# First layer's attention: the context values and probabilities split into high and low parts, and 512 keys in one product

## The chip, the cores and the metric

The kernel runs on one core of a Trainium2 chip. The metric is device microseconds of one execution. TensorE (PE in the profile) multiplies into PSUM, VectorE (DVE) and ScalarE (ACT) read PSUM and SBUF, SyncE's queue (SP) issues the transfers.

## The reference, cut to what matters

Two layers of a block with three token mixers (a gated linear recurrence, an mLSTM, a windowed attention), 512 latent tokens and 256 context tokens, width 2048, all in fp32. Only the attention is touched. It has 8 query heads of 128 channels; four heads share one key and value head (two of these).

```python
# latent tokens: a window of 128 to each side, and all 256 context keys
s_loc = einsum('bnqkgd,bnskd->bnkgqs', qb, kw) * scale      # masked to the window
s_ctx = einsum('bnqkgd,bckd->bnkgqc', qb, k_ctx) * scale
p = softmax(concatenate([s_loc, s_ctx, s_sink], axis=-1))
out = p[..., :span] @ vw + p[..., span:span + n_ctx] @ v_ctx
# context tokens (first layer only): the 256 context keys alone, and the sink
```

The result is `out * silu(cz)`. The context tokens' own attention is wanted in the first layer only, since the second layer is the last.

## The kernel before

**Layout.** Activations stand with channels on the 128 partitions and tokens along the free dimension: 512 latent tokens, two spare columns, 256 context tokens. A chunk is 128 tokens: 0 to 3 are latent, 4 and 5 context. Every projection (class `Proj`, method `mm`, L359) multiplies a 128-column weight tile by 512 and by 258 columns of activations, 16 times (the 16 slices of the width) and three times each: operands are cut into a high part of type fp32r and the rest, and high x high, high x low and low x high are summed. `load_w` (L318 to L322) fetches weights, ScalarE writes the high part, VectorE the low one; there are four buffers of each.

**The attention of one head** (`unit_c`): the query is projected, rotated (`rope`, its scratch tile from a ring of two buffers, tag `e`) and cut into two parts (`halves`, L1031 and L1032); then `attend` is called for three pairs of chunks. In the first layer these are (0, 3), (1, 4) and (2, 5), so there are 24 calls; in the second layer (0, 3), (1), (2). A latent chunk at the edge (0, 3) sees two local blocks of 128 keys, one in the middle (1, 2) three, a context chunk none; each sees the two context blocks, numbered 4 and 5.

**Inside `attend`:**
- the scores (L1051), three products of fp32r parts for each stretch of keys, into one PSUM tile `scps` of 1024 columns, the only buffer of its pool;
- the mask (L1057), row maximum (L1061), exponentials (L1070), their sum and its inverse, and the scaling of the probabilities `pr` (L1077);
- one transposition on TensorE for each chunk and block (L1084), four to a PSUM tile `ptps`, each tile copied to SBUF by ScalarE (L1085, tile `pt`, ring of two buffers, tag `z`);
- the values times the transposed probabilities, in fp32, one product of 128 columns for each chunk and block (L1091), into the PSUM tile `ops`; `ptps` and `ops` rotate through one pool of two buffers;
- the product with the gate on VectorE (L1093).

`values` turns the value head's 768 tokens so that keys stand on the partitions (`to_tokens`: transpositions at L635, ScalarE's copies at L636), into the tile `lvc`.

**Order.** Each engine's order of instructions is fixed when the program is built, by a planner that simulates the engines' times. It puts the attention's small pieces between the products of the projections that follow. Each engine then runs its list in that order and waits on semaphores.

Of the kernel before, what the change touches and what calls it, by code (L numbers as in the profile page):

```python
# [8 lines left out]
F32 = mybir.dt.float32  # L9
F32R = mybir.dt.float32r  # L10
I32 = mybir.dt.int32
AF = mybir.ActivationFunctionType
ALU = mybir.AluOpType
AX = mybir.AxisListType

P = 128
D = 2048
KT = 16
NL = 512
NC = 256  # L20
NT = NL + NC
XW = NL + 2 + NC
CO = NL + 2
# [5 lines left out]
COLP = [0, 128, 256, 384, CO, CO + 128]  # L29
# [26 lines left out]
def emit(tc, I, out, cfg=None, dbg=None):  # L56
# [5 lines left out]
    V, S, G, T = nc.vector, nc.scalar, nc.gpsimd, nc.tensor  # L62
# [8 lines left out]
    def sps(n, name):  # L71
        return psS.tile([P, 512], F32, tag="s", name=name)[:, 0:n]
# [22 lines left out]
    C_ = {}  # L95
# [438 lines left out]
    def run_units(l, last, up, mods):  # L534
# [5 lines left out]
        def U(i, name):  # L540
            return up.tile([P, 776], F32, tag=f"u{i}", name=name)

        def PAIR(i, name):
            return up.tile([P, 2, 776], F32, tag=f"p{i}", name=name)

        def Z(name):
            return up.tile([P, 776], F32, tag="z", name=name, bufs=2)
# [4 lines left out]
        def small(tag, n, bufs=2):  # L552
            return up.tile([P, n], F32, tag=tag, name=tag, bufs=bufs)
# [22 lines left out]
        def evac(nm, p, dst, extra=None, bias=True):  # L576

            with tc.high_priority():
                return evac_(nm, p, dst, extra, bias)
# [32 lines left out]
        def width(nm):  # L612
            return NL if is_lat(nm) else XW
# [10 lines left out]
        def to_tokens(src, dst, chunks, width_=P):  # L624

            two = isinstance(dst, list) and len(dst) == 2
            dst = dst if isinstance(dst, list) else [dst]
            for i, g in enumerate((chunks[0:4], chunks[4:6])):
                if not g:
                    continue  # L630
                t, c0 = (dst[i], g[0]) if two else (dst[0], 0)
                d = t[:, 0:(g[-1] + 1 - c0) * width_].rearrange("p (c w) -> p c w", w=width_)
                ps = sps(len(g) * P, "tps")
                for j, c in enumerate(g):
                    T.transpose(ps[:, j * P:j * P + P], src[:, COLP[c]:COLP[c] + P], C_["ident"])  # L635
                S.copy(out=d[:, g[0] - c0:g[0] - c0 + len(g), 0:P], in_=ps.rearrange("p (c w) -> p c w", w=P))  # L636

        ALLC = [0, 1, 2, 3, 4, 5]
# [396 lines left out]
        def every(t, c0, step, n, w=P):  # L1035

            return bass.AP(tensor=t.tensor, offset=t.offset + c0, ap=[tuple(t.ap[0]), (step, n), (1, w)])

        def attend(h, cs, q, kr, vt, m):


            n_ = len(cs)
            ps = psW.tile([P, 1024], F32, tag="w", name="scps")
            loc = [[b for b in (c - 1, c, c + 1) if 0 <= b < 4] if c < 4 else [] for c in cs]
            ns = [len(x) * P for x in loc]
            c0s = [512 - ns[0] if ns[0] > 256 else 0, 512 + NC if ns[0] > 256 else 512]
            w = [ps[:, c0:c0 + n + NC] for c0, n in zip(c0s, ns)]
            for c, x, lc, n in zip(cs, w, loc, ns):
                for k0, d0, len_ in ([(lc[0] * P, 0, n)] if lc else []) + [(CO, n, NC)]:
                    for i, (a, b) in enumerate(((0, 0), (0, 1), (1, 0))):  # L1050
                        T.matmul(x[:, d0:d0 + len_], q[:, a, COLP[c]:COLP[c] + P], kr[:, b, k0:k0 + len_],  # L1051
                                 start=(i == 0), stop=(i == 2))
            if ns[0] > 256:
                x, mask = every(w[0], 0, 2 * P, 2), C_["cmask"]
            else:
                x, mask = every(ps, P, 512 - P, 2), C_["cmask"][:, ::-1]
            V.tensor_tensor(out=x, in0=x, in1=mask, op=ALU.add)  # L1057
            sm = small("sm", 8, 4)
            mx, bi, su, si = (sm[:, 2 * i:2 * i + n_] for i in range(4))
            if n_ == 2 and ns[0] == ns[1]:  # L1060
                V.tensor_reduce(out=mx, in_=ps.rearrange("p (c k) -> p c k", c=2), axis=AX.X, op=ALU.max)  # L1061
            else:
                for i in range(n_):
                    V.tensor_reduce(out=mx[:, i:i + 1], in_=w[i], axis=AX.X, op=ALU.max)
            V.tensor_scalar(out=bi, in0=mx, scalar1=-SCALE, scalar2=C_["nsink"][:, l, h:h + 1],
                            op0=ALU.mult, op1=ALU.min)
            prs = []
            for i in range(n_):
                pr = U(8 + i, "pr")[:, 0:ns[i] + NC]
                S.activation(out=pr, in_=w[i], func=AF.Exp, scale=SCALE, bias=bi[:, i:i + 1],  # L1070
                             accum_out=su[:, i:i + 1])
                prs.append(pr)
            S.activation(out=si, in_=bi, func=AF.Exp, bias=C_["sink"][:, l, h:h + 1])
            V.tensor_tensor(out=su, in0=su, in1=si, op=ALU.add)
            V.reciprocal(out=su, in_=su)
            for i, pr in enumerate(prs):
                V.tensor_scalar(out=pr, in0=pr, scalar1=su[:, i:i + 1], scalar2=None, op0=ALU.mult)  # L1077
            blocks = [(i, j, kb) for i in range(n_) for j, kb in enumerate(loc[i] + [4, 5])]
            pts = []
            for a in range(0, len(blocks), 4):  # L1080
                g = blocks[a:a + 4]
                tp, pt = sps(len(g) * P, "ptps"), Z("pt")
                for k, (i, j, kb) in enumerate(g):
                    T.transpose(tp[:, k * P:k * P + P], prs[i][:, j * P:j * P + P], C_["ident"])  # L1084
                S.copy(out=pt[:, 0:len(g) * P], in_=tp)  # L1085
                pts += [pt[:, k * P:k * P + P] for k in range(len(g))]
            o = sps(n_ * P, "ops")
            for i in range(n_):
                mine = [(kb, pt) for (i_, _, kb), pt in zip(blocks, pts) if i_ == i]
                for k, (kb, pt) in enumerate(mine):  # L1090
                    T.matmul(o[:, i * P:i * P + P], vt[kb], pt, start=(k == 0), stop=(k == len(mine) - 1))  # L1091
            d = every(m, COLP[cs[0]], COLP[cs[-1]] - COLP[cs[0]] if n_ > 1 else P, n_)
            V.tensor_tensor(out=d, in0=o.rearrange("p (c k) -> p c k", k=P), in1=d, op=ALU.mult)  # L1093

        def unit_c():
            CS = PAIR(1, "cs")
            cosT, sinT = CS[:, 0, 0:NL], CS[:, 1, 0:NL]
            nc.sync.dma_start(cosT, I["cosT"])
            nc.sync.dma_start(sinT, I["sinT"])

            def values(g):
                nm = f"cv{g}"
                z = evac(nm, proj(nm), None if nm in early else U(5, "zcv"))
                if g == 0 or not last:
                    ts = [small("lvc", 1280, 1)[:, 0:NT]]
                else:
                    ts = [wp.tile([P, 512], F32, tag="st", name="cvt", bufs=7)[:, 0:n] for n in (NL, NC)]
                to_tokens(z, ts, ALLC)
                return [t[:, c:c + P] for t in ts for c in range(0, t.shape[1], P)]

            vts = []
            for h in range(8):
                g = h // 4
                if h % 4 == 0:
                    nm = f"ck{g}"
                    z = evac(nm, proj(nm), None if nm in early else U(7, "zck"))
                    rope(z, cosT, sinT)
                    kr = halves(z, 0, "ckr", XW)
                    vt = vts.pop(0) if vts else values(g)
                    if f"cv1" in ready:  # L1120
                        vts.append(values(1))
                nm, zn = f"cq{h}", f"cz{h}"
                q = evac(nm, proj(nm), None if nm in early else U((7, 5)[h % 2], "cq"))
                rope(q, cosT, sinT)
                q = halves(q, 2, "cqr", width(nm))
                m = evac(zn, proj(zn), None if zn in early else U(10 + h % 2, "cz"), bias=False)
                silu_bias(zn, m)
                for cs in ((0, 3), (1,), (2,)) if last else ((0, 3), (1, 4), (2, 5)):
                    attend(h, cs, q, kr, vt, m)
                nc.sync.dma_start(mixd[l][8 + h][:, 0:NL], m[:, 0:NL])  # L1130
                if not last:
                    nc.sync.dma_start(mixd[l][8 + h][:, NL:NT], m[:, CO:XW])
# [257 lines left out]
    for l in range(layers):  # L1390
        last = l == DEPTH - 1
# [131 lines left out]
```

## Time and profile before

| | us |
|---|---|
| time, median of 3 runs | 2804.38 (2802.26 to 2804.62) |
| the profiled execution | 2807.49 |
| its span | 2805.8 |
| TensorE busy | 2765.3 (99%) |
| VectorE busy | 1818.8 (65%) |
| ScalarE busy | 1180.6 (42%) |

The profile is of one execution, 2807.49 us long, some 3 us above the median. Busy times are inside its span. A matmul's row has a duration that reaches past the start of the next one, since matmuls are pipelined; what a matmul costs a full TensorE is the distance from its start to the next start. An fp32 product leaves two matmul records, an fp32r product and a transposition one. PEld is the load of the stationary operand, which runs beside the products.

### The profile page before, as it was taken

To read this page: it belongs to the slowest core of one execution; us is meant where nothing else is said; L and a number is where in the kernel's file an instruction comes from. 1 tells how busy PE (TensorE), PEld (TensorE's weight loads), DVE (VectorE), ACT (ScalarE), POOL (GpSimd) and SP (SyncE) were. 2 spreads that over 40 slices of the span, in tenths; PEclk is the share of its full clock that TensorE was granted. 3 is DMA by queue.
4 is the path that set the end of the run, shared out by engine and by line. 5 is a ranking of instruction groups with operands and counts; after the bars stand their busy time and mean duration, and the time that the engine had idled before them with its cause. 6 is when DMAs were issued, how large, how long until landed. Compare 5 with 4: busy or idle time off the path is not lost.

```text
span 2805.8 us, 53654 instructions
## 1 busy us (share of the span) xinstructions
PE 2765.3 (99%) x20833; PEld 2483.1 (88%) x20833; DVE 1818.8 (65%) x4163; ACT 1180.6 (42%) x2716; POOL 17.6 (1%) x32
## 2 busy tenths in 40 slices
PE   7999999999999999999999999999999999999998
PEld 4679879988888888889999999999899999999886
DVE  3436556764667778788777778566666665645526
ACT  3314324364453433324666644444444443333433
POOL 0000000000000000000000000000000000000000
PEclk8999999999999999999999999999999999999999
DMA  9771553321113144444767756224222222422535
GB/s 344 257 234 54 168 193 92 119 64 59 54 59 123 56 131 130 126 136 125 235 197 204 231 164 212 67 74 136 79 63 69 65 69 91 140 78 81 176 118 158
DMA packets 208144, 366.74 MB, mean 131 GB/s; under 512 B 24561, under 2 KB 42241, under 8 KB 207761
## 3 DMA queue, kind: packets, MB, share of 16 engines
q1 hardware_dynamic: 207888, 363.31, 41.1%
q8 instruction: 163, 2.67, 0.4%
q14 instruction: 93, 0.75, 0.1%
HBM read 344.94 MB, written 18.28 MB: 129 GB/s over the span
## 4 chain that ended last, share of the span: by engine, by line
PE 91%; DVE 2%; ACT 2%; DMA 1%; issue 1%; DVEq 0%; ACTq 0%; SPq 0%
PE pp L359 70%; PE pp L1345 6%; PE ops L1091 3%; PE scps L1051 2%; PE ptps L1084 1%; PE lv L799 1%; PE modps L246 1%; PE aops L885 1%; DMA raw<-in_wout 1%; PE tps L635 1%; PE sps L867 1%; PE nps L978 1%; PE cps L958 1%; PE nps L976 1%; PE ktps L851 0%
## 5 line engine op out<-in xcount | busy, mean ns | idle before, releaser
L359 PE MATMUL pp<-x0h,hi 128*128 128x256 f32 (+2 forms) x3088 | 942.2, 335 | 7.2 <-ACT x0h L410 5.2
L359 PE MATMUL pp<-x0l,hi 128*128 128x256 f32 (+2 forms) x3088 | 934.8, 332 | 0.1
L359 PE MATMUL pp<-x0h,lo 128*128 128x256 f32 (+1 forms) x3056 | 923.0, 332 | 0.7 <-DVE lo L322 0.7
L321 ACT CAST hi<-raw 128x512 fp32r<-128x512 f32 x764 | 473.0, 620 | 1042.8 <-PE pp L359 760.8
L322 DVE TENSOR_TENSOR lo<-raw,hi 128x512 fp32r<-128x512 f32 x764 | 526.6, 691 | 447.2 <-ACT hi L321 431.4
L359 PEld LDWEIGHTS pp<-x0h,hi 128*128 128x128 f32 x3088 | 544.8, 189 | 69.9 <-issue 6.9
L359 PEld LDWEIGHTS pp<-x0l,hi 128*128 128x128 f32 x3088 | 543.8, 189 | 59.2 <-issue 4.4
L359 PEld LDWEIGHTS pp<-x0h,lo 128*128 128x128 f32 x3056 | 537.1, 189 | 55.4 <-issue 2.5
L359 PE MATMUL pp<-x1h,hi 128*128 128x258 f32 (+1 forms) x1632 | 463.2, 284 | 1.4 <-ACT hi L321 1.3
L359 PE MATMUL pp<-x1l,hi 128*128 128x258 f32 (+1 forms) x1632 | 463.4, 284 | 0.1
L359 PE MATMUL pp<-x1h,lo 128*128 128x258 f32 (+1 forms) x1600 | 454.1, 284 | 0.6 <-DVE lo L322 0.4
L359 PEld LDWEIGHTS pp<-x1h,hi 128*128 128x128 f32 x1632 | 311.1, 191 | 7.8 <-issue 4.4
L359 PEld LDWEIGHTS pp<-x1l,hi 128*128 128x128 f32 x1632 | 309.2, 189 | 4.5 <-issue 3.6
L359 PEld LDWEIGHTS pp<-x1h,lo 128*128 128x128 f32 x1600 | 303.2, 190 | 6.5 <-issue 5.2
L270 DVE SCALAR_TENSOR_TENSOR mo<-st,sc,mo 128x512 f32<-128x512 f32 x150 | 112.8, 752 | 0.5
L270 DVE SCALAR_TENSOR_TENSOR scs<-st,sc,scs 128x512 f32<-128x512 f32 x150 | 112.8, 752 | 0.3
L1345 PE MATMUL pp<-lo,x0h 128*128 128x512 f32 x256 | 101.4, 396 | 0.0
L1345 PE MATMUL pp<-hi,x0h 128*128 128x512 f32 x256 | 100.9, 396 | 0.0
L1345 PE MATMUL pp<-hi,x0l 128*128 128x512 f32 x256 | 100.8, 395 | 0.0
L1085 ACT COPY pt<-ptps 128x512 f32<-128x512 f32 x96 | 47.7, 516 | 122.6 <-PE ptps L1084 122.0
L813 ACT COPY lvc<-aqq 128x256 f32<-128x256 f32 x140 | 60.3, 431 | 84.3 <-DVE aqq L822 63.4
L819 DVE TENSOR_TENSOR akk<-akk,aff 128x256 f32<-128x256 f32 x168 | 76.5, 455 | 12.2 <-PE ktps L851 9.4
(381 smaller groups left out, 3006.4 us busy)
## 6 DMA issues: line engine op xcount, KB each, us to landing
raw<-in_win SPq DMA_DIRECT2D x500, 256.0 KB, 2.7
st<-in_wmod SPq DMA_DIRECT2D x288, 256.0 KB, 3.4
raw<-in_wout SPq DMA_DIRECT2D x192, 256.0 KB, 3.3
mw<-in_wmod SPq DMA_DIRECT2D x96, 256.0 KB, 5.2
raw<-in_wlast SPq DMA_DIRECT2D x80, 256.0 KB, 3.1
st<-in_win SPq DMA_DIRECT2D x24, 256.0 KB, 4.5
xr<-in_xin SPq DMA_DIRECT2D x48, 128.0 KB, 3.3
st<-mixd SPq DMA_DIRECT2D x45, 128.0 KB, 2.7
```

The costliest lines, as they stand in the source:

```text
L246: prev = T.matmul(ps[32 * j:32 * j + 32, :], scs[:, 32 * kt:32 * kt + 32], ws[j], start=(i == 0 and (side or g == 0)), stop=(i == 1 and (s ...
L270: V.scalar_tensor_tensor(out=acc, in0=w, scalar=c, in1=acc, op0=ALU.mult, op1=ALU.add)
L321: S.copy(out=hi, in_=raw)
L322: lo_ins[:] = [V.tensor_tensor(out=lo, in0=raw, in1=hi.bitcast(F32), op=ALU.subtract).ins]
L359: T.matmul(dst, self.w[w][:, kt % 4, :], xs[o][kt][j][:, x0:x0 + n], start=(first and i == 0 and (self.outs is None or self.outs[k][1])), ...
L635: T.transpose(ps[:, j * P:j * P + P], src[:, COLP[c]:COLP[c] + P], C_["ident"])
L813: S.copy(out=mixed(qm.unsqueeze(1), 0, 256, b, 0), in_=mixed(Q2, c0, 256, b))
L819: V.tensor_tensor(out=x, in0=x, in1=blocks(F2, c0, b, b, 776, True), op=ALU.mult)
L1051: T.matmul(x[:, d0:d0 + len_], q[:, a, COLP[c]:COLP[c] + P], kr[:, b, k0:k0 + len_], start=(i == 0), stop=(i == 2))
L1085: S.copy(out=pt[:, 0:len(g) * P], in_=tp)
L1091: T.matmul(o[:, i * P:i * P + P], vt[kb], pt, start=(k == 0), stop=(k == len(mine) - 1))
L1345: x = T.matmul(ps[c], xs[0][kt][a][:, c * P:c * P + P], w[b].rearrange("p a b -> p (a b)"), start=(kt == kts[0] and i == 0), stop=(kt == k ...
```

## The change

In the first layer (`not last`), and nowhere else:

- **Scores.** For a chunk with 256 local keys (chunks 0 and 3) the local and the context keys, two stretches of 256 columns, become the moving operand of one product of 512 columns: 6 products in place of 12 in the call (0, 3). The other two calls keep theirs.
- **Context values.** `values` transposes the same six chunks, but the two context blocks get a PSUM tile, a copy into an fp32r high part and a VectorE subtraction for the low part (tile `vc`); the four local blocks go to `lvc` as before.
- **Context probabilities.** The four transpositions of the two context blocks for both chunks of a call go first, into one PSUM tile, block by block with the two chunks side by side. ScalarE copies it into an fp32r high part (tag `z`), VectorE subtracts for the low part (`ptl`, tag `e`, the ring that `rope` and the gates' scratch use too). The local blocks are transposed and copied after it as before.
- **Values times probabilities.** For each context block three fp32r products of 256 columns (both chunks at once) take the place of two fp32 products of 128 columns. They come first into `ops`; the local blocks' fp32 products add to them.

```diff
-                for k0, d0, len_ in ([(lc[0] * P, 0, n)] if lc else []) + [(CO, n, NC)]:
+                for k0, d0, len_ in [(lc[0] * P, 0, 2 * NC)] if n == NC else ([(lc[0] * P, 0, n)] if lc else []) + [(CO, n, NC)]:
                     for i, (a, b) in enumerate(((0, 0), (0, 1), (1, 0))):
-                        T.matmul(x[:, d0:d0 + len_], q[:, a, COLP[c]:COLP[c] + P], kr[:, b, k0:k0 + len_],
+                        keys = every(kr[:, b], k0, CO - k0, 2, NC) if n == NC else kr[:, b, k0:k0 + len_]
+                        T.matmul(x[:, d0:d0 + len_], q[:, a, COLP[c]:COLP[c] + P], keys,
                                  start=(i == 0), stop=(i == 2))
...
-            blocks = [(i, j, kb) for i in range(n_) for j, kb in enumerate(loc[i] + [4, 5])]
+            blocks = [(i, j, kb) for i in range(n_) for j, kb in enumerate(loc[i] + ([4, 5] if last else []))]
             pts = []
+            if not last:
+                tp = sps(4 * P, "ptps")
+                for k in range(2):
+                    for i in range(2):
+                        j = len(loc[i]) + k
+                        T.transpose(tp[:, (2 * k + i) * P:(2 * k + i) * P + P], prs[i][:, j * P:j * P + P], C_["ident"])
+                both = up.tile([P, 776], F32R, tag="z", name="pt", bufs=2), up.tile([P, 776], F32R, tag="e", name="ptl", bufs=2)
+                S.copy(out=both[0][:, 0:4 * P], in_=tp)
+                V.tensor_tensor(out=both[1][:, 0:4 * P], in0=tp, in1=both[0][:, 0:4 * P].bitcast(F32), op=ALU.subtract)
...
             o = sps(n_ * P, "ops")
+            if not last:
+                for k in range(2):
+                    for j, (a, b) in enumerate(((0, 0), (0, 1), (1, 0))):
+                        T.matmul(o, vt[4 + k][a], both[b][:, 2 * k * P:2 * k * P + 2 * P], start=(k + j == 0),
+                                 stop=(k + j == 3 and not blocks))
...
+                if not last:
+                    t = small("lvc", 1280, 1)
+                    to_tokens(z, t, ALLC[0:4])
+                    ps = sps(NC, "tps")
+                    for j in range(2):
+                        T.transpose(ps[:, j * P:j * P + P], z[:, CO + j * P:CO + j * P + P], C_["ident"])
+                    vc = up.tile([P, 2, NC], F32R, tag="vc", name="vc")
+                    hi, lo = vc[:, 0], vc[:, 1]
+                    S.copy(out=hi, in_=ps)
+                    V.tensor_tensor(out=lo, in0=ps, in1=hi.bitcast(F32), op=ALU.subtract)
```

## Rows read from the trace of the kernel before

**Rows 1.** The page: busy time of each engine, share of the span, instructions.

```profile
PE 2765.3 (99%) x20833; PEld 2483.1 (88%) x20833; DVE 1818.8 (65%) x4163; ACT 1180.6 (42%) x2716; POOL 17.6 (1%) x32
```

**Rows 2.** The chain that ended last, by engine, whole span; then 205 to 570 us.

```profile
PE 91%; DVE 2%; ACT 2%; DMA 1%; issue 1%; DVEq 0%; ACTq 0%; SPq 0%
...
by line: PE pp L359 68.9%; PE ops L1091 10.8%; PE scps L1051 8.7%; PE ptps L1084 5.4%; PE modps L246 4.4%; PE modp L194 0.4%; PE pp L375 0.4%; DVE zg L595 0.3%; PE tps L635 0.3%; ACT Lg L679 0.2%; PE shps L523 0.2%; DVE zg L600 0.1%; issue 
```

**Rows 3.** Busy times by stretch: from:to, length, PE, PEld, DVE, ACT, POOL, clock, DMA.

```profile
210.00:570.00 360.00, 360.00 (x2328) 311.85 (x2329) 220.73 (x455) 131.29 (x268) 1.50 (x2) 1.00 0.39 125
570.00:1340.00 770.00, 766.94 (x5979) 678.75 (x5978) 567.38 (x1325) 321.81 (x859) 9.30 (x16) 1.00 0.31 97
1340.00:1600.00 260.00, 256.00 (x2135) 253.71 (x2135) 198.99 (x475) 167.71 (x361) 0.00 (x0) 1.00 0.72 220
```

**Rows 4.** L1091 and L1051 in 210 to 570 us: records, duration ns min/median/max, forms.

```profile
L1091 PE MATMUL ops<-pt,lvc x352: 269/275/276, 230.3 to 566.1; 128*128 128x128 f32 x176
...
L1051 PE MATMUL scps<-ckr,cqr x240: 275/285/442, 213.8 to 549.7; 128*128 128x256 f32 x96, 128*128 128x384 f32 x24
```

**Rows 5.** Timeline of PE: start, length, engine, line, operation. Twelve scores, then projections.

```profile
213.79 1.60 PE L1051 MATMUL scps<-ckr,cqr 128*128 128x256 f32 x12
...
215.23 0.28 PE L359 MATMUL pp<-x1l,hi 128*128 128x258 f32 x1
```

**Rows 6.** Timeline of PE: the value products of a call, projections around them.

```profile
227.19 0.28 PE L359 MATMUL pp<-x1h,lo 128*128 128x258 f32 x1
227.31 0.39 PE L359 MATMUL pp<-x0h,hi 128*128 128x512 f32 x1
...
230.35 1.95 PE L1091 MATMUL ops<-pt,lvc 128*128 128x128 f32 x16
232.05 0.36 PE L359 MATMUL pp<-x1h,lo 128*128 128x258 f32 x1
232.25 0.40 PE L359 MATMUL pp<-x0h,hi 128*128 128x512 f32 x1
```

**Rows 7.** Timeline of PE, last projection: 512-column fp32r products, first and last of 14.

```profile
2649.77 0.39 PE L1345 MATMUL pp<-hi,x0h 128*128 128x512 f32 x1
...
2652.78 0.39 PE L1345 MATMUL pp<-lo,x0h 128*128 128x512 f32 x1
```

**Rows 8.** DVE by line and shape: count, busy us, mean ns, idle before and releaser.

```profile
L648 DVE TENSOR_TENSOR mix<-mixps,ag 128x512 f32<-128x512 f32 x8 | 5.5, 688 | 14.6 <-PE mixps L646 14.6
L650 DVE TENSOR_TENSOR mix<-mixps,ag 128x256 f32<-128x256 f32 x4 | 1.7, 414 | 0.0
```

**Rows 9.** Timeline, second call of head 0: transpositions, copies, value products.

```profile
235.48 0.93 PE L1084 MATMUL ptps<-c_ident,pr 128*128 128x128 f32 x7
...
240.13 1.72 PE L1091 MATMUL ops<-pt,lvc 128*128 128x128 f32 x14
241.60 1.56 PE L1051 MATMUL scps<-ckr,cqr 128*128 128x256 f32 x11
```

**Rows 10.** Timeline of PE, ACT and DVE, third call: the same, close together.

```profile
243.01 0.60 PE L1084 MATMUL ptps<-c_ident,pr 128*128 128x128 f32 x4
...
243.70 0.59 ACT L1085 COPY pt<-ptps 128x512 f32<-128x512 f32 x1 [4.37 <-PE ptps L1084]
...
244.23 1.23 DVE L1061 TENSOR_REDUCE sm<-scps 128x2 f32<-128x1024 f32 x1
245.62 0.96 DVE L595 TENSOR_TENSOR cq<-pp,rb 128x770 f32<-128x770 f32 x1 [0.17 <-PE pp L359]
...
245.42 1.73 PE L1091 MATMUL ops<-pt,lvc 128*128 128x128 f32 x14
```

**Rows 11.** Waits of PE from 570 to 2800 us: total us, times, longest.

```profile
PE pp L359 <- ACT hi L321: 2.6, 4, 1.1
PE gtps L734 <- ACT PF L724: 2.4, 2, 1.9
PE gtps L734 <- DVE gT L735: 2.3, 2, 1.2
PE pp L359 <- DVE lo L322: 1.1, 3, 0.7
```

**Rows 12.** VectorE's low parts of weights: by shape, and two that follow each other.

```profile
L322 DVE TENSOR_TENSOR lo<-raw,hi 128x512 fp32r<-128x512 f32 x764 | 526.6, 691 | 447.2 <-ACT hi L321 431.4 <-ACT pt L1085 5.9 <-DMA st<-x1d 3.0
...
215.70 0.69 DVE L322 TENSOR_TENSOR lo<-raw,hi 128x512 fp32r<-128x512 f32 x1
...
219.71 0.69 DVE L322 TENSOR_TENSOR lo<-raw,hi 128x512 fp32r<-128x512 f32 x1
```

## What was predicted before the change was run

> **What bounds the kernel now.** I read the engines' busy times first: TensorE is busy for 99% of the span, VectorE for 65%, ScalarE for 42% [rows 1]. The chain that ended last says the same from the other side: 91% of it is TensorE's own work [rows 2]. An average hides stages, so the next view is the stretch in which the first layer's attention runs, 210 to 570 us, by the first and last value product and score [rows 4]: there TensorE is busy for 360.00 of 360.00 us at the full granted clock (1.00, which is 2.4 GHz), while VectorE works 220.73 us and ScalarE 131.29 us and the transfers take 0.39 of the DMA engines [rows 3]. The chain through this stretch is TensorE's lines one after another: the projections' products 68.9%, value products 10.8%, scores 8.7%, transpositions 5.4% [rows 2]. The reader is to see that TensorE never waits here, because the planner has put the attention between projections that are ready anyway. So a microsecond of product time taken out of this stretch is a microsecond off the end, and latency inside the attention costs nothing as long as TensorE has other products in its list. What counts is therefore the price of a product on a full TensorE, which is the distance between starts, not the duration in its row.
>
> **Prices.** Twelve scores of 256 columns take from 213.79 to 215.23 us [rows 5]: 1.44/12 = 0.120 us each. Fourteen starts of 512-column fp32r products lie between 2649.77 and 2652.78 us [rows 7]: 3.01/13 = 0.2315 us each. For the fp32 value product: from the start of the first of 16 records to the second projection product behind them, 230.35 to 232.25 us, there are 1.90 us, and one of the products in between is a 258-column one, which costs 0.12 us (227.19 to 227.31) [rows 6]. So 8 value products cost 1.78 us, 0.2225 us each. I take the distance across the following product because the start of the one behind a group of fp32 records is shifted.
>
> **The change part by part.** *Context values times probabilities:* each of the 24 calls loses four fp32 products, 4 x 0.2225 = 0.890 us, and gets six fp32r products of 256 columns, 6 x 0.120 = 0.720 us. That the row has 352 records, two for each of 8 x (8 + 7 + 7) = 176 products, confirms the count [rows 4]. Gain: 24 x 0.170 = 4.1 us. No row shows an fp32r product with these operands; the nearest are the 256-column scores at 0.120 and the 258-column projections at 0.12, and the best the columns allow is half of the 512-column price, 0.116. With 0.116 the gain is 24 x 0.194 = 4.7 us, with 0.1225 (0.0025 above the scores) it is 24 x 0.155 = 3.7 us. I take 0.120, since the new products also come in a row with one stationary load each, as the scores do.
>
> *Scores of the call (0, 3):* 8 calls lose twelve products of 256 columns, 1.44 us, and get six of 512, 6 x 0.2315 = 1.389 us. Gain: 8 x 0.051 = 0.4 us. The moving operand is now two runs of 256 columns with a gap; no row shows such a product. If each costs what two of 256 do, the gain is 0; if the gap costs as much again as the whole joint saves (0.0085 us a product), it is a loss of 0.4 us. I take the contiguous price: it is the only row of that width.
>
> Here a rule speaks about the size. The Trainium skill, "TensorE: Matmul & The Clock Gate", section "Back-to-back issue gap", gives a gap of N/2.4 + 2.5 ns at full clock, 109.2 ns at 256 columns and 215.8 ns at 512. By that rule an estimate of this edit's gain is 8 x (12 x 0.1092 - 6 x 0.2158) = 0.1 us in place of 0.4. The rows here are dearer (0.120 and 0.2315), and they decide.
>
> *Transpositions:* 8, 7 and 7 before and after; only their order changes. Cost 0.
>
> *ScalarE:* the copies out of `ptps` keep their number (two a call) and their sizes. Cost 0.
>
> *VectorE:* one subtraction of 512 columns out of PSUM more in each call, at the 0.688 us of the nearest form with a PSUM operand, and two of 256 columns at 0.414 us for the values [rows 8]: 24 x 0.688 + 2 x 0.414 = 17.3 us. VectorE is idle for 360.00 - 220.73 = 139 us of the stretch [rows 3], so this I cost at nothing; the work that hides it is the projections' products on TensorE. If that cover were gone it would cost up to 0.688 us in each call (below).
>
> *Waits that are added:* the second of the six products needs the low part, and `ops` needs the buffer that the subtraction is the last to read. On TensorE everything behind that product waits, the next projection's products too. The low parts also take turns in the ring of two that `rope` and the gate's scratch use, so the rotation of the next head's query can start only when the second call's value products are done. That puts some 4 us of rotation and splitting behind them, which TensorE covers with projections that are already in its list. No transfer is added or moved.
>
> **The sum.** 4.1 + 0.4 = 4.5 us, all on TensorE's path. Against the profiled execution: 2807.49 - 4.5 = 2803.0. That execution is 3.1 us above the median of the runs, so in the metric: 2804.38 - 4.5 = 2799.9 us. The bounds of the unknown prices give a gain of 3.7 - 0.4 = 3.3 to 4.7 + 0.4 = 5.1 us, 2799.3 to 2801.1 us. A planner that is given other instructions also orders others differently; I allow 2 us for that to each side: 2797.3 to 2803.0.
>
> **The rivals.**
> *TensorE waits for the low part (slower).* The place is the second context product of each call. In the third call the four transpositions started at 243.01, the copy ended at 243.70 + 0.59 = 244.29, and the first value product started at 245.42 [rows 10]; but VectorE was in a reduction from 244.23 to 245.46. A subtraction behind it would end at about 246.2, so the product, left in its place, would wait some 0.8 us. VectorE's next row starts only at 245.62, behind the reduction [rows 10]. The Trainium skill, "PSUM — Partial Sum Buffer", section "Engine vs sequencer instructions", calls VectorE's queue strict FIFO; by that rule the wait could not be dodged, and the rows agree. At the full price, 0.8 us in all 24 calls, this costs 19 us: 2804.4 - 4.5 + 19 = 2819 us. It makes the kernel slower (by over 5.6 us) from an average wait of (4.5 + 5.6)/24 = 0.42 us a call. Against it: in the second call the transpositions began at 235.48 and the value products only at 240.13 [rows 9], room for the subtraction; and the planner counts the subtraction when it places the products. No value product waits for its copies today.
>
> *The gain is eaten in part.* The same wait in every third call, 8 x 0.6 = 5 us, or a weight's low part late behind VectorE's new work: about 2804.4 us, no change. Against the second: a weight's low part is cast about every 4 us (215.70, 219.71) with 0.691 us of work [rows 12] and four buffers, so VectorE may fall back by some 12 us before TensorE runs out.
>
> *The new order also removes waits elsewhere.* Behind the attention TensorE still waits for parts of weights and for the gates, 2.6 + 2.4 + 2.3 + 1.1 = 8.4 us in all [rows 11]. They depend on how the lists interleave. If half of them go, the time is 2799.9 - 4.2 = 2795.7 us. Against it: nothing in the change aims at them, and new ones are as likely.
>
> *The 512-key product is not one product for the engine.* Then only the 0.4 us is lost: 2800.3 us, inside the forecast's bounds.
>
> **How the numbers follow.** About 0.2%, 5.6 us, is what a measurement of this kernel can tell from no change; faster means below 2798.8 us, slower above 2810.0 us. The forecast (2797.3 to 2803.0) has 0.62, and of that some 0.16 lies below 2798.8. The removed waits (below 2797.3) have 0.16, the eaten gain (2803 to 2810) 0.14, the wait for the low part (above 2810) 0.08. So faster 0.16 + 0.16 = 0.32, same 0.46 + 0.14 = 0.60, slower 0.08. The likeliest is the forecast, 2799.9 us, which lies within 0.2%. The range reaches to half of the removed waits and to the first 2 us of the eaten gain: 2795.7 to 2805.0.
>
> **What would show it right or wrong.** Right: in the first layer's stretch the value products' records fall from 352 to 160, with 144 fp32r ones beside them at 0.120 us from start to start; 48 score records fewer; TensorE still without idle time, and the stretch shorter by 4 to 5 us. Wrong: idle time of TensorE ahead of the context products with the subtraction as releaser; a distance of more than 0.24 us between 512-key scores; or a change of TensorE's waits behind 570 us as large as the gain itself.

## The result, and the profile after

The change made the kernel slower: 2825.83 us (2825.52 to 2827.74) against 2804.38 us, a ratio of 1.0077 with a 95% interval of 1.0067 to 1.0088. That is 21.5 us more where 4.5 us less was forecast.

One statement made ahead of the prediction was wrong: the score edit is not tied to the first layer. It holds wherever a chunk has 256 local keys, so in the second layer's calls (0, 3) too: 16 calls, not 8.

The page of the kernel after, its busy times (as rows 1):

```profile
PE 2772.4 (98%) x20689; PEld 2481.0 (88%) x20689; DVE 1834.3 (65%) x4189; ACT 1180.5 (42%) x2717; POOL 17.6 (1%) x32
```

TensorE has 144 records fewer, as the change says, and yet it is busy for 7 us more. The stretches show where. Busy times of the kernel after, with columns as in rows 3, up to 545 us, through the place of the loss, and behind it:

```profile
210.00:545.00 335.00, 329.58 (x2038) 280.16 (x2037) 193.59 (x390) 117.24 (x238) 0.74 (x1) 0.99 0.36 115
545.00:582.00 37.00, 23.22 (x113) 20.20 (x112) 34.80 (x72) 11.13 (x22) 0.74 (x1) 0.72 0.41 117
582.00:640.00 58.00, 56.74 (x443) 49.01 (x441) 38.99 (x93) 34.79 (x63) 0.00 (x0) 1.00 0.24 74
```

From 545 to 582 us TensorE is busy for 23.22 of 37 us, with a granted clock of 0.72, while VectorE is full (34.80). Most of the loss shows here: counted by the projections' products (L359), the kernel after is 1.7 us ahead of the one before at the 2050th (544.1 against 545.8 us), 22.8 us behind at the 2100th (583.4 against 560.6), and 19 us behind at the end. (The profiled execution of the kernel before was itself 3 us longer than its median.) What TensorE waits for in this stretch (total us, times, longest):

```profile
PE scps L1053 <- ACT pr L1072: 8.8, 1, 8.8
PE ptps L1088 <- DVE pr L1079: 2.3, 2, 1.7
PE ops L1103 <- ACT pt L1097: 1.9, 2, 1.1
PE ops L1103 <- DVE ptl L1091: 0.8, 1, 0.8
```

These are the steps of the last head's calls, one after another: scores wait for exponentials, transpositions for probabilities, value products for copies. The timeline of TensorE there, cut:

```profile
552.55 0.60 PE L194 MATMUL modp<-c_ident,scs 128*128 128x128 f32 x4
561.98 2.61 PE L1053 MATMUL scps<-ckr,cqr 128*128 128x384 f32 x9 [8.82 <-ACT pr L1072]
566.25 0.45 PE L1088 MATMUL ptps<-c_ident,pr 128*128 128x128 f32 x1 [1.67 <-DVE pr L1079]
...
568.98 0.58 PE L1103 MATMUL ops<-pt,vc 128*128 128x256 f32 x1 [0.79 <-ACT pt L1097]
570.34 0.58 PE L1103 MATMUL ops<-ptl,vc 128*128 128x256 f32 x1 [0.77 <-DVE ptl L1091]
...
573.13 2.15 PE L1053 MATMUL scps<-ckr,cqr 128*128 128x384 f32 x9
...
578.41 0.80 PE L359 MATMUL pp<-x0h,hi 128*128 128x512 f32 x1
```

Between 552.55 and 578.41 us there is no projection product at all. In the kernel before the attention's pieces lay between projections [rows 6]; here none is left to run. The reason stands on VectorE's timeline. The last head's query leaves PSUM at 491.32 us, and its rotation starts at 543.23, right behind the third call's subtraction of the head before:

```profile
491.32 0.96 DVE L595 TENSOR_TENSOR cq<-pp,rb 128x770 f32<-128x770 f32 x1
...
539.98 0.42 DVE L1110 TENSOR_TENSOR cz<-ops,cz 128x256 f32<-128x256 f32 x1 [1.74 <-PE ops L1108]
540.39 0.69 DVE L322 TENSOR_TENSOR lo<-raw,hi 128x512 fp32r<-128x512 f32 x1
542.51 0.69 DVE L1091 TENSOR_TENSOR ptl<-ptps,pt 128x512 fp32r<-128x512 f32 x1 [1.43 <-ACT pt L1090]
543.23 0.69 DVE L1023 TENSOR_TENSOR rope<-cq,cs 64x512 f32<-64x512 f32 x1
```

The same query in the kernel before (timeline of VectorE):

```profile
499.72 0.95 DVE L595 TENSOR_TENSOR cq<-pp,rb 128x770 f32<-128x770 f32 x1
...
501.95 0.69 DVE L1023 TENSOR_TENSOR rope<-cq,cs 64x512 f32<-64x512 f32 x1
```

Before, 2.2 us lie between the two; after, 51.9 us. That is not itself the price, since the head before has its own first scores only at 511.15 us. The price stands between two heads: from the third scores of the first head to the first scores of the second there were 8.0 us before (233.64 to 241.60 [rows 9]), and there are 18.1 us after (230.59 to 248.64).

```profile
242.90 0.69 DVE L1091 TENSOR_TENSOR ptl<-ptps,pt 128x512 fp32r<-128x512 f32 x1
243.62 0.69 DVE L1023 TENSOR_TENSOR rope<-cq,cs 64x512 f32<-64x512 f32 x1
248.64 1.22 PE L1053 MATMUL scps<-ckr,cqr 128*128 128x512 f32 x2 [3.48 <-ACT cqr L1031]
```

So the rotation stands behind the third call's subtraction at the first change of head too, and TensorE runs out of work there as well: the projections have no product between 241.58 and 249.66 us. Up to 545 us TensorE is idle for 5.42 us (335.00 less 329.58), 3.48 us of it here; the kernel before had no idle time there [rows 3]. The count of projection products hides this loss, because the attention is later at that count than it was before.

Back to the last head. The next mixer's first query projection is written over the keys' tile (both are the pair with number 0), so it stays in its PSUM buffer until the last scores are done: it leaves at 577.40 us, behind the scores of 573.13.

```profile
577.40 0.95 DVE L595 TENSOR_TENSOR aqq<-pp,rb 128x770 f32<-128x770 f32 x1
```

The gates' projection holds the other buffer of that pool. It leaves by a copy into a tile (`zg`) of the ring in which the turned probabilities stand (tag `z`), and the copy waits for a call's value products:

```profile
594.60 0.80 ACT L372 COPY zg<-pp 128x770 f32<-128x770 f32 x1 [3.50 <-PE ops L1103]
```

So TensorE has no place for a third projection. This is theory R: the ring that the low parts share with the rotation makes the heads follow one another where they used to overlap, the attention falls behind the projections, and the lateness is paid where TensorE's list runs out, above all beside the last head.

### The profile page after: what moved, and what is told of

Read it like the earlier page. It is cut to its first block, busy times and chain, and to the rows that moved or that the text cites. A ratio compares the mean times of both kernels' runs of the same rounds, so it can differ in the third digit from the quotient of the medians.

```text
span 2824.8 us, 53370 instructions
## 1 busy us (share of the span) xinstructions
PE 2772.4 (98%) x20689; PEld 2481.0 (88%) x20689; DVE 1834.3 (65%) x4189; ACT 1180.5 (42%) x2717; POOL 17.6 (1%) x32
## 4 chain that ended last, share of the span: by engine, by line
PE 90%; DVE 3%; ACT 2%; DMA 1%; issue 0%; SPq 0%; DVEq 0%; ACTq 0%
PE pp L359 70%; PE pp L1374 6%; PE scps L1053 2%; PE ops L1108 2%; PE lv L799 1%; PE modps L246 1%; PE aops L885 1%; PE ptps L1096 1%; PE tps L635 1%; PE sps L867 1%; PE nps L978 1%; PE cps L958 1%; PE nps L976 1%; PE ops L1103 1%; PE ktps L851 0%
## 5 line engine op out<-in xcount | busy, mean ns | idle before, releaser
L359 PE MATMUL pp<-x0h,hi 128*128 128x256 f32 (+2 forms) x3088 | 942.2, 335 | 7.1 <-ACT x0h L410 5.1
L359 PE MATMUL pp<-x0l,hi 128*128 128x256 f32 (+2 forms) x3088 | 935.3, 333 | 0.1
L359 PE MATMUL pp<-x0h,lo 128*128 128x256 f32 (+1 forms) x3056 | 922.0, 332 | 0.3 <-DVE lo L322 0.3
L359 PEld LDWEIGHTS pp<-x0h,hi 128*128 128x128 f32 x3088 | 545.6, 189 | 70.7 <-ACT x0h L410 6.8
L359 PEld LDWEIGHTS pp<-x0l,hi 128*128 128x128 f32 x3088 | 544.2, 189 | 60.1 <-issue 5.2
L359 PEld LDWEIGHTS pp<-x0h,lo 128*128 128x128 f32 x3056 | 537.1, 189 | 54.6 <-issue 1.7
L359 PE MATMUL pp<-x1h,hi 128*128 128x258 f32 (+1 forms) x1632 | 463.7, 285 | 0.2 <-ACT hi L321 0.2
L359 PE MATMUL pp<-x1l,hi 128*128 128x258 f32 (+1 forms) x1632 | 463.7, 284 | 0.1
L359 PE MATMUL pp<-x1h,lo 128*128 128x258 f32 (+1 forms) x1600 | 453.6, 284 | 0.4 <-DVE lo L322 0.4
L359 PEld LDWEIGHTS pp<-x1h,hi 128*128 128x128 f32 x1632 | 311.1, 191 | 7.7 <-issue 5.2
L359 PEld LDWEIGHTS pp<-x1l,hi 128*128 128x128 f32 x1632 | 309.4, 190 | 7.4 <-issue 6.1
L359 PEld LDWEIGHTS pp<-x1h,lo 128*128 128x128 f32 x1600 | 303.3, 190 | 6.8 <-issue 5.2
L1053 PE MATMUL scps<-ckr,cqr 128*128 128x384 f32 (+2 forms) x336 | 73.7, 349 | 12.5 <-ACT pr L1072 9.0
```

The costliest lines, as they stand in the source:

```text
L359: T.matmul(dst, self.w[w][:, kt % 4, :], xs[o][kt][j][:, x0:x0 + n], start=(first and i == 0 and (self.outs is None or self.outs[k][1])), ...
```

## The experiments

Each is given against the runs of the kernel before on the same chip (medians 2804.56 for the first four, 2805.17 for the next four, 2805.49 for three, 2804.54 for the last). The rivals of R: L, the subtraction's own latency and VectorE's extra work lengthen the attention; P, it is the planner's other order and VectorE's modulation sums in the last head's chain.

**The low parts outside the ring** (one half in free columns of the high part's tile; room is made by letting a scratch tile share another's tag):

```diff
-both = up.tile([P, 776], F32R, tag="z", name="pt", bufs=2), up.tile([P, 776], F32R, tag="e", name="ptl", bufs=2)
+pt = up.tile([P, 776], F32R, tag="z", name="pt", bufs=2)
+ptl = up.tile([P, NC], F32R, tag="ptl", name="ptl", bufs=1)
+both = [(pt[:, k * NC:k * NC + NC], (pt[:, 4 * P:4 * P + NC], ptl)[k]) for k in range(2)]
```

> The changed kernel with the low parts of the probabilities outside the ring of two that the rotation and the gate use: one half stands in the unused columns of the high part's tile, the other in a tile of its own, so the subtraction is two of 256 columns. Theory R (the shared ring puts the next head's rotation behind this head's attention, and the attention runs late against the projections): the rotation of a head follows its query's evacuation within 3 us again, no idle time of TensorE near 550 us, and the gain of the products shows: 2797 to 2802 us. Rival L (the subtraction's own latency and VectorE's extra work lengthen the attention): still 2818 us or more. Rival P (the planner's other order, VectorE's modulation sums in the last head's chain): anything from 2805 to 2826 us.

2802.56 us, ratio 0.9992 (0.9983 to 1.0001), 0.6 us above R's range. The loss of the change is gone with every one of its products and subtractions in place. L falls; P is not excluded by this run alone, since the planner's order differs too.

**The kernel before with the ring shared, and nothing else:**

```diff
-tp, pt = sps(len(g) * P, "ptps"), Z("pt")
+tp, pt = sps(len(g) * P, "ptps"), E_("pt") if a == 0 and not last else Z("pt")
```

> The kernel before, with one edit: in the first layer the first tile of turned probabilities of each call is taken from the ring that the rotation and the gate use, and not from its own; no instruction is added or taken away. Theory R: the same loss as the change without its gain, 2815 to 2835 us, with TensorE idle near 550 us. Rival L: no change, 2802 to 2806 us, since nothing is subtracted. Rival P: no change beyond 3 us.

2808.11 us, 1.0012 (1.0002 to 1.0021): 3.5 us, far less than R's 10 us or more. Sharing alone is not enough; as first put, R was wrong. The last head's rotation starts at 512.18 us here, right behind the second call's product with the gate at 511.72: ten microseconds later than before, not forty.

**The score edit alone:**

```diff
+joint = n == NC
-for k0, d0, len_ in ([(lc[0] * P, 0, n)] if lc else []) + [(CO, n, NC)]:
+for k0, d0, len_ in [(lc[0] * P, 0, 2 * NC)] if joint else ([(lc[0] * P, 0, n)] if lc else []) + [(CO, n, NC)]:
...
```

> The kernel before with the score edit alone (512 keys in one product; it holds in both layers, 16 calls). By the prices of the rows, 16 x 0.051 = 0.8 us less: 2803.6 us; starts of 512-key products 0.23 us apart. If the two runs of keys cost what two products do: 2804.4 us and 0.24 us. All theories expect no loss here.

2804.13 us, 1.0000 (0.9991 to 1.0009): too small to be told from nothing. The price shows in the timeline of TensorE, six products from 213.38 to 214.77 us, 0.232 us each:

```profile
213.38 1.56 PE L1053 MATMUL scps<-ckr,cqr 128*128 128x512 f32 x6
214.77 0.28 PE L359 MATMUL pp<-x1l,hi 128*128 128x258 f32 x1
```

**The changed kernel with fewer modulation sums on VectorE in this stretch:**

```diff
-PACE = ({"c": 0.7, "a": 0.2, "b": 1.2}, ...
+PACE = ({"c": 0.2, "a": 0.4, "b": 1.2}, ...
```

> The changed kernel with fewer of the second layer's modulation sums on VectorE during the first layer's attention (pace 0.2 in place of 0.7; the next mixer takes 0.4 in place of 0.2). Theory R: the last head's chain runs faster, but starts as late; at most the 9 us of its longest wait go: 2815 to 2826 us. Rival P: most of the loss goes, 2800 to 2808 us. Rival L: little change, 2820 to 2826 us.

2823.84 us, 1.0068 (1.0053 to 1.0084), 2 us below the changed kernel. The total hides two parts. Behind the attention, at the 2400th projection product, this kernel is 10.6 us behind the one before, where the changed kernel is 22.7 us behind: 12 us were won. Some 7 us come back near 1370 us, at the end of the layer, where the sums that were put off are made up. So VectorE's sums in the last head's chain carry a part of the loss at that place (P), and R's "at most 9 us" was too low. The last rotation still starts at 542.17 us: the lateness itself is not theirs.

**The rotation outside the ring, the low parts in it:**

```diff
-t = E_("rope")
+t = E_("rope")[:, 0:NL] if last else None
+t = h2(t) if last else spare[0]
...
 cosT, sinT = CS[:, 0, 0:NL], CS[:, 1, 0:NL]
+spare[:] = [CS[:, :, NL:NL + NC]]
```

> The changed kernel with one edit: in the first layer the rotation's scratch stands in the unused columns of the tile of cosines and sines, so the rotation needs no buffer of the shared ring; the low parts and the gate's scratch still share it, and no instruction is added. Theory R: it is the rotation's place behind the second and third call that costs the time, so the loss goes: 2798 to 2804 us. If the ring costs the time through the gate's scratch, or through VectorE's subtractions: 2815 us or more.

2800.57 us, 0.9985 (0.9977 to 0.9994), 4.6 us below the kernel before. The rotation's buffer is the place: low parts and the gate's scratch may share the ring, and nothing is lost. (The planner orders this kernel anew too, so the run names the origin of the loss, and not how much of it comes by way of the order.) Here the stretch is full again (columns as in rows 3):

```profile
545.00:582.00 37.00, 36.93 (x225) 32.43 (x224) 22.91 (x47) 15.08 (x25) 0.00 (x0) 1.00 0.37 111
```

225 records in the 37 us in which the changed kernel has 113.

**The kernel before with one VectorE step more in each call, its output in the ring:**

```diff
+if a == 0 and not last:
+    src, pt = pt, E_("pt2")
+    V.tensor_tensor(out=pt[:, 0:4 * P], in0=tp, in1=src[:, 0:4 * P], op=ALU.max)
```

> The kernel before, its products and their number as they were; in the first layer the first tile of turned probabilities of each call goes through one more VectorE operation of 512 columns out of PSUM (the shape of the subtraction), whose output stands in the shared ring until the value products have read it. Theory R in the form that the ring and the longer call cost the time together: 2815 to 2835 us, as in the change, though none of its products is here. If the fp32r products or their places in TensorE's list are part of the cause: below 2812 us.

2816.63 us, 1.0044 (1.0029 to 1.0059): 11.5 us, near the foot of R's range and above the 2812 us that would have given the new products a part (four runs, 2813.58 to 2820.00). The last rotation waits as in the change, behind the third call's step:

```profile
524.38 0.69 DVE L1088 TENSOR_TENSOR pt<-ptps,pt 128x512 f32<-128x512 f32 x1 [0.69 <-ACT pt L1085]
525.10 0.69 DVE L1023 TENSOR_TENSOR rope<-cq,cs 64x512 f32<-64x512 f32 x1
```

**The same step, its output in a tile of its own:** `E_("pt2")` becomes `small("pt2", 512, 1)`.

> As the run with the step and the ring, but the operation's output stands in a tile of its own. Theory R: the step alone is hidden, 2803 to 2807 us. Rival L (the step's own latency): 2815 us or more.

2805.48 us, 1.0001 (0.9992 to 1.0010). So, on the kernel before: the ring alone costs 3.5 us, the step alone 0.3 us, both together 11.5 us. The two act together, because a call that is longer holds the ring longer and the step stands ahead of the rotation on the same engine.

**The rotation outside the ring and the scores as before:** the previous edit of the rotation, and the lines of the score edit undone.

> The changed kernel with the rotation's scratch outside the ring and the scores as they were before (two products of 256 keys, not one of 512). The value products' gain alone remains, some 4 us by the rows: 2799 to 2803 us; within 1 us of the run with the joint scores, since a product of two runs of keys cost 0.24 us.

2801.22 us, 0.9987 (0.9978 to 0.9996): the value products alone bring 4.0 us; the joint scores are not seen.

**The ring for half of the heads** (the rotation's scratch in the ring for heads 0 to 3 only, then for heads 4 to 7 only):

```diff
-t = E_("rope")
...
+t = spare[0] if not last and h >= 4 else h2(E_("rope")[:, 0:NL])
```

> The changed kernel with the rotation's scratch in the shared ring for heads 0 to 3 alone, and in the unused columns of the cosines' tile for heads 4 to 7. Theory R with its second half (what is lost is lateness of the attention against the projections, paid once, where the last head finds no projections left): the later heads catch up and the loss is small, 2799 to 2806 us. If every call that waits costs TensorE its own time: half of the loss, 2808 to 2818 us.

2808.24 us, 1.0010 (1.0001 to 1.0020).

> The same the other way round: the ring for heads 4 to 7 alone. Theory R with lateness paid at the end: lateness gathered in the last four heads has no time to be made good, 2808 to 2826 us, clearly later than with the ring for heads 0 to 3; the last head's scores end after 556 us. If every waiting call costs its own time: as the other run, 2808 to 2818 us.

2813.78 us, 1.0029 (1.0018 to 1.0039). The order is the one that R expected: the ring costs more in the last four heads. But the first run was to stay under 2806 us, and both lie inside the rival's 2808 to 2818 us, so the times alone do not refute the rival, and R's "paid once" is too simple. The traces show where each kernel pays. With the ring in heads 0 to 3 TensorE waits 3.48 us at 248.88 us for the second head's split query, as in the changed kernel; it is idle for 5.30 us between 205 and 545 us, with a granted clock of 0.77 from 245 to 260 us, and for 0.99 us between 545 and 582 us. With the ring in heads 4 to 7 these are 1.25 and 4.06 us; without any sharing, 1.27 and 0.07 us. So the first heads' loss (7.7 us above the 2800.57 us without sharing) is for the most part paid at once, at the first change of head, and the last heads' loss at the end: each where the list runs out.

**The changed kernel with the scores in two products again:** the lines of the score edit undone.

> The changed kernel with the scores of 256 local and 256 context keys as two products again. If the joint product, and the places the planner finds for it, has no part in the loss: 2822 to 2828 us. If it has: below 2820 us.

2827.58 us, 1.0080 (1.0063 to 1.0097): the joint product has no part in the loss.

**The changed kernel with the keys' tile and the cosines' exchanged:**

```diff
-CS = PAIR(1, "cs")
+CS = PAIR(1 if last else 0, "cs")
...
-kr = halves(z, 0, "ckr", XW)
+kr = halves(z, 0 if last else 1, "ckr", XW)
```

> The changed kernel, ring and all, with two tiles exchanged in the first layer: the keys' parts take the place of the cosines and sines and the other way round. The next mixer's first projection is written where the keys were in the changed kernel, so there it waits for the last scores; here it waits for the last rotation only, and TensorE gets one projection more to run (some 16 us of products) while the last head's calls go on. Theory R with lateness paid where no projection is left: a large part of the loss goes although the attention is as late as before, 2806 to 2816 us. If lateness costs by itself, or the waits inside the calls do: 2820 to 2828 us.

2816.27 us, 1.0043 (1.0026 to 1.0060). The attention is as late as in the changed kernel (last rotation 542.48 us, last scores 576.51), but the next projection can leave PSUM at 553.34 us, and TensorE takes up another one:

```profile
551.82 0.60 PE L194 MATMUL modp<-c_ident,scs 128*128 128x128 f32 x4
554.35 0.50 PE L359 MATMUL pp<-x0h,hi 128*128 128x512 f32 x1 [1.93 <-DVE aqq L595]
```

The stretch of this kernel, with columns as in rows 3:

```profile
545.00:582.00 37.00, 33.61 (x198) 29.78 (x197) 34.27 (x72) 11.89 (x24) 0.74 (x1) 0.95 0.43 132
```

The 25.9 us without a projection are down to a wait of 1.93 us, the stretch holds 198 records in place of 113, and 9.6 us of the loss are gone, 0.3 us short of R's range. At the last head it is the missing projections that turn lateness into time. Of the 11.7 us that are left a part has another place, which the exchange does not touch: the wait at the first change of head is here too (3.47 us at 248.73 us), and TensorE is idle for 5.52 us between 205 and 545 us.

Lateness and time beside each other (times of start in us, from the profiled executions; the last head is head 7; the last column is the median, on chips whose medians of the kernel before lie between 2804.4 and 2805.5):

| kernel | last rotation | last scores | next query leaves PSUM | time |
|---|---|---|---|---|
| before | 501.95 | 548.50 | 555.96 | 2804.4 |
| step, own tile | 501.31 | 549.53 | 554.65 | 2805.5 |
| low parts outside the ring | 491.20 | 537.57 | 553.64 | 2802.6 |
| rotation outside the ring | 494.76 | 544.08 | 552.70 | 2800.6 |
| before, ring shared | 512.18 | 548.50 | 557.61 | 2808.1 |
| ring for heads 0 to 3 | 495.57 | 553.89 | 559.36 | 2808.2 |
| ring for heads 4 to 7 | 523.90 | 555.48 | 558.43 | 2813.8 |
| step in the ring | 525.10 | 557.84 | 562.45 | 2816.6 |
| fewer sums on VectorE | 542.17 | 564.23 | 566.41 | 2823.8 |
| changed | 543.23 | 573.13 | 577.40 | 2825.8 |
| changed, tiles exchanged | 542.48 | 576.51 | 553.34 | 2816.3 |

Large lateness and long times go together, but not row by row: with the ring shared on the kernel before, the last scores are no later (548.50 us), and the time is 3.5 us longer.

## Why the prediction was wrong, point by point

**What bounds the kernel:** right. TensorE was full, and time that was taken from its list came off the end wherever it stayed full.

**Prices of the products:** right. Six context products in a row, from the timeline of the kernel after:

```profile
546.40 0.28 PE L1103 MATMUL ops<-pt,vc 128*128 128x256 f32 x1
546.52 0.28 PE L1103 MATMUL ops<-ptl,vc 128*128 128x256 f32 x1
546.64 0.40 PE L1103 MATMUL ops<-pt,vc 128*128 128x256 f32 x2
546.88 0.28 PE L1103 MATMUL ops<-ptl,vc 128*128 128x256 f32 x1
546.99 0.28 PE L1103 MATMUL ops<-pt,vc 128*128 128x256 f32 x1
547.11 0.28 PE L359 MATMUL pp<-x1h,hi 128*128 128x258 f32 x1
```

From 546.40 to 547.11 us that is 0.71/6 = 0.118 us each; 0.120 was taken. The forecast gain of 4.5 us is what the same products give without the loss: 4.6 us with the rotation outside the ring (interval 0.6 to 2.3 thousandths, 1.7 to 6.5 us, so that the agreement to 0.1 us is luck). The joint score was priced at 0.2315 us and cost 0.232; its term would have been 16 x 0.051 = 0.8 us, since it holds in 16 calls. The rule of the Trainium skill weighed there ("TensorE: Matmul & The Clock Gate", "Back-to-back issue gap") gives 0.2158 us; the measurement stands.

**VectorE's subtractions at nothing:** right in the sense meant, work beside TensorE's: the step with a tile of its own cost 0.3 us, inside what can be told from nothing.

**The added waits:** this step failed. The text named the ring and the place ("the rotation of the next head's query can start only when the second call's value products are done"), and then put "some 4 us of rotation and splitting behind them, which TensorE covers with projections that are already in its list". Two things in that sentence were wrong. It priced the rotation's own length, not the overlap that is lost: from the third scores of the first head to the next head's first scores there were 8.0 us and are now 18.1, and the last head's rotation, which ran 2.2 us after its query, now runs 51.9 us after it. And it took the cover as given for every head, from a stretch that was full [rows 3], without asking how long TensorE's list is where it is shortest: at the first change of head (a wait of 3.48 us) and beside the last head (13.78 us without work). What would have told is not a busy time but the tiles: the next mixer's query is written where the keys stand, the gates' projection waits for a place in the ring of the probabilities, so the list holds two more projections and no third. The prediction asked for the cost if the cover is gone only for the subtraction's 0.688 us.

**The rivals:** the slower one had the right sign and the wrong place. It put the loss into each call's second context product, up to 0.8 us in 24 calls. In all, TensorE's products of L1103 waited 0.8 us for the subtraction (once) and 2.6 us for the local copies; the two longest waits, 8.82 us (scores for exponentials) and 3.48 us (scores for a split query), are not ahead of those products. Its reason against, "the planner counts the subtraction", held; TensorE's list simply had nothing else to offer in those places. Of the other rivals, the removed waits say more of one execution than of the change: between the 6000th projection product (1352 us) and the end every other trace of this document gains 1.4 to 4.6 us on the trace before, whatever was edited. The 512-key product is one product for the engine (0.232 us).

**What stays open.** On the kernel before, ring and step together cost 11.5 us; the change loses 21.5 us and the 4.6 us that it should have won. The table shows that its attention is later still (last scores 573.13 against 557.84 us), and the run with fewer sums shows VectorE's modulation sums in the last chain as one contributor, by 12 us at that place. The wait at the first change of head is another, some 6 us by the estimate below. How much of the remainder is the planner's choice to put the rotation behind the third call's subtraction was not tried apart.

The best of these kernels is the change with the rotation's scratch in the unused columns of the cosines' tile: 2800.57 us, 0.9985 (0.9977 to 0.9994) of the kernel before. The same kernel without the joint scores (2801.22 us) cannot be told from it.

## What to carry to other kernels

A new tile in an old ring costs what the ring's other users did ahead of time: list them in program order, and for each ask what it will now wait for and how early it used to run. An attention hidden between projections is hidden only while there are projections whose outputs have a place; look at the first change of head and at the last head, and at which tiles the next stage writes first. And where one engine is full, price lateness at the next point where its list runs out, not where it arises.

## What the runs showed of the hardware

In this kernel, time without work cost TensorE twice: the wait itself, and slower products behind it. In the kernel after, nine scores in a row took 1.41 us from 531.45 us on, with a full engine around them; nine of the same form took 2.61 us from 561.98 us on, behind the 8.82 us without work.

```profile
531.45 1.41 PE L1053 MATMUL scps<-ckr,cqr 128*128 128x384 f32 x9
```

The granted clock around the wait of 3.48 us at 248.64 us, and of the stretches behind the long gap, with columns as in rows 3:

```profile
245.00:260.00 15.00, 11.52 (x51) 9.48 (x50) 8.62 (x15) 4.92 (x8) 0.00 (x0) 0.77 0.10 33
560.00:578.00 18.00, 11.06 (x48) 9.67 (x48) 17.32 (x38) 5.66 (x15) 0.00 (x0) 0.59 0.47 141
578.00:582.00 4.00, 4.00 (x14) 3.41 (x15) 4.00 (x8) 0.00 (x0) 0.00 (x0) 0.57 0.53 129
582.00:600.00 18.00, 18.00 (x113) 15.76 (x111) 6.54 (x14) 5.05 (x11) 0.00 (x0) 1.00 0.35 111
```

Full clock is 2.4 GHz and the lower level 1.2 GHz, or 0.5 in this column, so 0.59 and 0.57 mean the lower level for most of these stretches, and 0.77 for a little under half of the first. Between 578 and 582 us TensorE is busy throughout and still runs so. The products there, from its timeline:

```profile
579.21 0.63 PE L359 MATMUL pp<-x0l,hi 128*128 128x512 f32 x1
579.86 0.63 PE L359 MATMUL pp<-x0h,lo 128*128 128x512 f32 x1
580.50 0.63 PE L359 MATMUL pp<-x0h,hi 128*128 128x512 f32 x1
...
581.62 0.40 PE L359 MATMUL pp<-x0h,lo 128*128 128x512 f32 x1
581.97 0.40 PE L359 MATMUL pp<-x0h,hi 128*128 128x512 f32 x1
```

A pair of products (512 and 258 columns) comes every 0.64 us until 581.14 us and every 0.35 us from 581.62 us on; the ratio, 0.55, is that of the scores too (1.41/2.61 = 0.54). An estimate of what the clock took: TensorE is busy for 15.06 us between 560 and 582 us (11.06 + 4.00), at a clock of 0.585 in the mean; the same work at full clock would be 15.06 x 0.585 = 8.8 us, so 6.3 us went to the clock. The idle time from 545 to 582 us is 13.78 us (37.00 less 23.22). Together that is 20 of the 24.5 us by which the kernel fell back here (from 1.7 us ahead to 22.8 behind). By the same estimate the first change of head cost 3.48 us of waiting and 11.52 x 0.23 = 2.6 us of clock. No run held the clock up over such a gap, so the split is an estimate, not an experiment.

A moving operand of two runs of 256 columns with a gap between them, as in the joint score, cost 0.232 us; a contiguous one of 512 columns cost 0.2315 us [rows 7]. No cost of the gap is seen.
